# Plain scatters into rows of their own, the last two blocks summed from SBUF, and a head with two-column products

## The chip, the cores and the metric

One core of a Trainium2 chip runs the whole program once. The metric is device time in microseconds (us). The engines are TensorE (PE, matrix products), VectorE (DVE), ScalarE (ACT), GpSimd (POOL) and SyncE (SP, here mostly an issuer of transfers); 16 DMA engines move data between DRAM and on-chip memory (SBUF), for all queues together.

## What is computed

One layer of a decoder trunk on 1024 tokens of width 1024, all in float32: adaLN modulation, an input projection, dilated attention beside a depthwise convolution, an output projection, and then a mixture of experts, with a final norm:

```python
mod = silu(c) @ w_mod + b_mod                  # six vectors of 1024
h = rms_norm(x, g_norm1) * (1 + sc1) + sh1
u = h @ w_in                                   # q, k, v, ga, gb
x = x + gt1 * (concat([attention(q, k, v), conv(ga, gb)]) @ w_out)
h2 = rms_norm(x, g_norm2) * (1 + sc2) + sh2
# per token: one of 4 groups, in it the top 2 of 8 experts, weights w
x = x + gt2 * sum_over_the_two(w * (silu(h2 @ w_gate[e]) * (h2 @ w_up[e])) @ w_down[e])
out = rms_norm(x, g_final)
```

## The kernel before

**Head.** TensorE makes shift and scale of the first norm, two vectors in four halves of 512, as products of `ca` with blocks of w_mod (`mod_mm`, L129), lying in rows. To turn them into columns it multiplies by single columns of the identity: four halves j by eight k, 32 products of one column (L190). VectorE makes s1 and a1 of them (L192 to L194). Behind that `h_half` turns the normed x by 4 transposes for each of 8 k and two halves (L203), and ScalarE writes hT from them (L205).

**Projections and attention.** The products of hT with w_in go on from about 41 us (L268 to L270). POOL's queue loads further blocks of w_mod in that stage (L122). Then attention, convolution on VectorE, output projection, second norm and the routing tables follow, up to about 640 us.

**Experts.** 32 experts, sorted by load; each has three matrices of 2 MB. They pass through a ring of eight buffers of 2 MB (`ring` L578, `eload` L588): SP issues two loads of 1 MB for each matrix, in one fixed order (`uses`), and each issue waits for its buffer and for the transfer eight issues before. Experts in the list PK (13 of them, 64 tokens at most) use F32 products (L1035, L1104); the others split the weights into a rounded part and a rest on ScalarE and VectorE (L102, L105) and use three fp32r products each (L1046 to L1048, L1122 to L1124). For each expert POOL gathers the tokens' rows from `h2d` (`gather`, L931) and, at its end, `scatter` (L1089) adds the scaled result `ys` (L1135) into `x1d` in DRAM: an indirect transfer with `compute_op=OP.add`. Two tokens' experts may meet in a row of x1d, so each scatter waits for the one before. The order of TensorE, VectorE and ScalarE in this stage is written by hand; SP and POOL follow in program order.

**Overflow and end.** `tc.If(nov > j)` (L1360) covers experts with more tokens than fit; `nov` is 0 here, so the branch is not taken, but it stands in the program. After it, for each of 8 tiles of 128 tokens: SP loads a tile of x1d (L1390), ScalarE sums its squares (L1392), POOL makes 1/rms in two steps (L93, L94), VectorE scales (L1394), and ScalarE's queue writes it out (L1395).

Of the kernel before, what the change touches and what calls it, by code (L numbers as in the profile page):

```python
# [35 lines left out]
PK = (4, 6, 8, 10, 12, 14, 16, 18, 20, 23, 25, 28, 31)  # L36
C0, C1 = 2, 3
# [6 lines left out]
def trunk_kernel(ctx, tc, x, c, w_mod, b_mod, g_norm1, w_in, conv_w, conv_b, conv_ln_g, conv_ln_b,  # L44
# [15 lines left out]
    h2d = dram.tile([T, D], F32, name="h2d")  # L60
    x1d = dram.tile([T, D], F32, name="x1d")
# [124 lines left out]
    pc0 = pbank(psT)  # L186
# [5 lines left out]
    nc.vector.tensor_add(s1, pc0[:, 0:8], bm[:, 0, :])  # L192
    nc.vector.scalar_tensor_tensor(a1, pc0[:, 8:16], 1.0, bm[:, 1, :], op0=OP.add, op1=OP.add)
# [5 lines left out]
    def h_half(half):  # L199
        for k in range(8):  # L200
            pt = pbank(psT)
            for i in range(4):
                nc.tensor.transpose(pt[:, i * P:(i + 1) * P], xn[half * 4 + i][:, k:D:8], ident)  # L203
# [47 lines left out]
    modp = tc.alloc_tile_pool(name="modp", bufs=2, side="right")  # L251

# [457 lines left out]
    early_t, late_t = [[rtc.tile([P, n], dt, name=f"{nm}{n}") for nm, dt in (("ti", I32), ("ws", F32))]  # L710
                       for n in (LO, E - LO + 1 + NOV)]

    half_t = [rtc.tile([P, E - LO + 1], dt, name=f"{nm}h") for nm, dt in (("ti", I32), ("ws", F32))]
# [8 lines left out]
    def tables(tb, dst, pool, halves=False):  # L722

        ti, ws = dst
# [182 lines left out]
    gt2b = tabp.tile([P, D], F32, name="gt2b")  # L907
    caps = tabp.tile([E, 2], F32, name="caps")
    pos = tabp.tile([1, E + 1], I32, name="pos")
    ovr = tabp.tile([1, NOV], I32, name="ovr")  # L910
    moe = tc.alloc_tile_pool(name="moe", bufs=2, side="right", reuse_waits="tile")
# [12 lines left out]
    todo = []  # L924

# [163 lines left out]
    def scatter(ys, si, n):  # L1089

        nc.gpsimd.indirect_dma_start(  # L1091
# [4 lines left out]
    def down(e):  # L1096
# [359 lines left out]
```

## Time and profile before

| | us |
|---|---|
| median of 3 runs | 1183.0 (1182.07 to 1186.11) |
| the profiled execution | 1183.84 |
| its span | 1182.0 |
| TensorE busy | 1081.5 (91% of the span) |
| VectorE busy | 784.1 (66%) |
| ScalarE busy | 513.0 (43%) |
| POOL busy | 224.3 (19%) |

All times of the profile are in us from the span's start. TensorE is busy for most of the span, but the limits differ by stage: near the start it waits for w_mod, in the experts' stage all 16 DMA engines are busy, and at the end TensorE has nothing to do at all. A row of a timeline gives the start, the length, the engine (PEld is TensorE's weight load, an engine name with q its queue's sequencer), the line, the operation with output<-input, and the count of merged instructions.

### The profile page before, as it was taken

The page shows a single profiled execution, that of the slowest core. Times are in us where ns is not written, and L with a number is a line of the kernel's source. Part 1 is how long each engine was busy: PE and PEld are TensorE (multiplying, and loading weights), DVE is VectorE, ACT ScalarE, POOL GpSimd, SP SyncE. Part 2 cuts the span into 40 slices and gives each one's busy share as a digit, 9 for nine tenths or more (in the row PEclk, how much of TensorE's full clock was granted, in tenths as well). Part 3 has the DMA queues.
Part 4 walks back from the last instruction along what each step waited for, and adds up shares of the span by engine and source line. Part 5 has one row for each costly group of instructions (what it writes and reads, how often), then busy time and mean ns, then how long its engine had stood idle before and what let it go on. Part 6 is the DMA issues. An engine that isn't in the chain of part 4 may idle for free. (4 is left out here: it accounts for less than half of the span.)

```text
span 1182.0 us, 16081 instructions
## 1 busy us (share of the span) xinstructions
PE 1081.5 (91%) x5896; PEld 790.6 (67%) x5896; DVE 784.1 (66%) x1303; ACT 513.0 (43%) x800; POOL 224.3 (19%) x202
## 2 busy tenths in 40 slices
PE   3899999999799999999889999999979999898970
PEld 0667777778565666788678877777656677576740
DVE  1457999993666556777669766666654587485833
ACT  2431112111777665322257655554553475364613
POOL 2340000002412202300111222222111231221112
PEclk8799999999798999999979999999989999999995
DMA  9632634302011004744868999999999999999948
GB/s 367 207 139 94 240 116 145 111 30 89 1 37 36 1 1 173 287 183 162 324 222 302 357 398 408 406 399 384 392 391 384 386 389 369 380 402 373 395 129 294
DMA packets 60828, 292.65 MB, mean 248 GB/s; under 512 B 11861, under 2 KB 16213, under 8 KB 33092
## 3 DMA queue, kind: packets, MB, share of 16 engines
q1 hardware_dynamic: 48020, 253.16, 54.8%
q0 software_dynamic: 11296, 34.17, 10.1%
q10 hardware_dynamic: 1424, 4.20, 0.9%
q8 instruction: 48, 0.79, 0.3%
q14 instruction: 40, 0.33, 0.1%
HBM read 275.75 MB, written 26.23 MB: 255 GB/s over the span
## 5 line engine op out<-in xcount | busy, mean ns | idle before, releaser
L105 DVE TENSOR_TENSOR elo<-raw,ehi 128x1024 fp32r<-128x1024 f32 x228 | 271.0, 1221 | 91.9 <-ACT ehi L102 90.0
L102 ACT CAST ehi<-raw 128x1024 fp32r<-128x1024 f32 x228 | 234.1, 1049 | 98.9 <-DMA raw<-in_w_exp_down_dram 33.1
L317 DVE SCALAR_TENSOR_TENSOR cv<-cv,cwT 128x1024 f32<-128x1024 f32 x120 | 154.1, 1284 | 3.6
L269 PE MATMUL pb<-hT,whi 128*128 128x512 f32 x256 | 101.2, 395 | 1.7 <-POOL hT L98 1.3
L268 PE MATMUL pb<-hT,whi 128*128 128x512 f32 x256 | 102.5, 402 | 0.0
L270 PE MATMUL pb<-hT,wlo 128*128 128x512 f32 x256 | 101.0, 395 | 0.1
L1122 PE MATMUL py<-ehi,hh 128*128 128x512 f32 x152 | 64.5, 424 | 7.1 <-ACT ehi L102 5.6
L1091 POOL DMA_INDIRECT x1d<-ys,ti x19 | 42.6, 2240 | 132.3 <-DVE ys L1135 117.2
L1123 PE MATMUL py<-elo,hh 128*128 128x512 f32 x152 | 62.8, 413 | 2.7 <-DVE elo L105 2.6
L268 PEld LDWEIGHTS pb<-hT,whi 128*128 128x128 f32 x256 | 48.5, 189 | 21.9 <-ACT whi L102 9.2
L1124 PE MATMUL py<-ehi,hl 128*128 128x512 f32 x152 | 62.0, 408 | 0.9 <-DVE hl L105 0.9
L1046 PE MATMUL pg<-ehi,xh 128*128 128x512 f32 x152 | 61.6, 405 | 0.4 <-ACT xh L102 0.4
L1047 PE MATMUL pu<-elo,xh 128*128 128x512 f32 x152 | 60.2, 396 | 0.4 <-DVE elo L105 0.4
L1048 PE MATMUL pg<-ehi,xl 128*128 128x512 f32 x152 | 59.9, 394 | 0.3 <-DVE xl L105 0.3
L1046 PE MATMUL pu<-ehi,xh 128*128 128x512 f32 x152 | 59.9, 394 | 0.0
L1048 PE MATMUL pu<-ehi,xl 128*128 128x512 f32 x152 | 59.8, 393 | 0.0
L1047 PE MATMUL pg<-elo,xh 128*128 128x512 f32 x152 | 59.7, 393 | 0.0
L269 PEld LDWEIGHTS pb<-hT,whi 128*128 128x128 f32 x256 | 48.5, 190 | 13.1 <-POOL hT L98 2.9
L1035 PE MATMUL pu<-raw,x 128*64 128x256 f32 x448 | 51.6, 381 | 5.5 <-DMA raw<-in_w_exp_up_dram 5.5
L270 PEld LDWEIGHTS pb<-hT,wlo 128*128 128x128 f32 x256 | 48.5, 190 | 10.4 <-DVE wlo L105 0.6
L422 ACT ACTIVATE ns<-ns,st 128x128 f32<-128x128 f32 (+7 forms) x64 | 49.2, 772 | 11.1 <-DVE st L418 10.5
L931 POOL DMA_INDIRECT xe<-h2d,ti x20 | 29.5, 1474 | 128.0 <-PE pt L1015 90.1
(284 smaller groups left out, 2197.3 us busy)
## 6 DMA issues: line engine op xcount, KB each, us to landing
raw<-in_w_exp_gate_dram SPq DMA_DIRECT2D x64, 1024.0 KB, 22.6
raw<-in_w_exp_up_dram SPq DMA_DIRECT2D x64, 1024.0 KB, 23.4
raw<-in_w_exp_down_dram SPq DMA_DIRECT2D x64, 1024.0 KB, 22.8
wm<-in_w_mod_dram POOLq DMA_DIRECT2D x16, 1024.0 KB, 5.2
wm<-in_w_mod_dram SPq DMA_DIRECT2D x8, 1024.0 KB, 9.5
raw<-in_w_in_dram SPq DMA_DIRECT2D x3, 2048.0 KB, 9.8
xt<-in_x_dram SPq DMA_DIRECT2D x8, 512.0 KB
raw<-in_w_in_dram SPq DMA_DIRECT2D x4, 1024.0 KB, 12.6
```

The source lines that it names most:

```text
L102: nc.scalar.copy(hi, src)
L105: nc.vector.tensor_sub(lo, src, hi.bitcast(F32))
L268: nc.tensor.matmul(p[half], hi[:, k, :], hT[0][:, k, sl], start=(k == 0), stop=False)
L269: nc.tensor.matmul(p[half], hi[:, k, :], hT[1][:, k, sl], start=False, stop=False)
L270: nc.tensor.matmul(p[half], lo[:, k, :], hT[0][:, k, sl], start=False, stop=(k == 7))
L317: nc.vector.scalar_tensor_tensor(y, u[:, j:j + T], w, y, op0=OP.mult, op1=OP.add)
L1046: nc.tensor.matmul(o, xh[:, k, :], hi[:, kk, :], start=(k == 0), stop=False)
L1047: nc.tensor.matmul(o, xh[:, k, :], lo[:, kk, :], start=False, stop=False)
L1048: nc.tensor.matmul(o, xl[:, k, :], hi[:, kk, :], start=False, stop=(k == 7))
L1122: nc.tensor.matmul(o, hh[:, k, :], hi[:, half, :], start=(k == 0), stop=False)
L1123: nc.tensor.matmul(o, hh[:, k, :], lo[:, half, :], start=False, stop=False)
L1124: nc.tensor.matmul(o, hl[:, k, :], hi[:, half, :], start=False, stop=(k == 3))
```

## The change

Three parts.

**Head.** The 32 one-column products become 16 with two columns each (`ident[:, 32 * h:P:64]`), whose results land in neighbouring columns. Five of the first half's eight groups of transposes (`x_turned`) are placed by hand between the w_mod products.

**Scatters.** A new DRAM buffer `ybuf` has two rows per token, one for each chosen expert. It is zeroed in the projections' stage by eight transfers of 1 MB on POOL's queue from one small tile. A scatter now writes plainly to row 2*token + choice; the tables get a second index `si` for it. The scatters are declared independent of each other.

**End.** The results of the last two experts (30 and 31, `LATE`) are not scattered; they stay in SBUF, split into two fp32r parts, and one-hot matrices S (`late_tokens`) say which token each row belongs to. SP loads all of x1d (2 transfers of 2 MB) and ybuf (8 of 1 MB) into ring buffers behind the last weights, ahead of the branch. After the branch, for each tile: two rows of ybuf are added to x1d, on VectorE for even tiles (`fin_v`) or by F32 products with the identity on TensorE for odd ones (`fin_y`); eight fp32r products add the late results (`fin_late`); VectorE adds the sum from PSUM (`fin_add`), and square, 1/rms, scaling and the write follow (`fin_out`, the write on SP's queue).

```diff
@@ head
+    def x_turned(half, k, pool):
+        pt = pbank(pool)
+        for i in range(4):
+            nc.tensor.transpose(pt[:, i * P:(i + 1) * P], xn[half * 4 + i][:, k:D:8], ident)
+        return pt
-    for k in range(8):
-        mod_mm(pm, mod_load(nc.sync, xp, 0, k, 4), k)
+    with tc.manual_schedule(engines={mybir.EngineType.PE}):
+        for k in range(8):
+            mod_mm(pm, mod_load(nc.sync, xp, 0, k, 4), k)
+            if k > 2:
+                turned[0, k - 3] = x_turned(0, k - 3, ps1)
-    for j in range(4):
-        c0 = 8 * (j // 2)
-        for k in range(8):
-            nc.tensor.matmul(pc0[64 * (j % 2):64 * (j % 2) + 64, c0 + k:c0 + k + 1], mrow[:, k:512:8],
-                             ident[:, 32 * j:32 * j + 1], start=True, stop=True, skip_group_check=True)
+    for k in range(8):
+        for h in range(2):
+            nc.tensor.matmul(pc0[64 * h:64 * h + 64, 2 * k:2 * k + 2], mrow[:, k:512:8],
+                             ident[:, 32 * h:P:64], start=True, stop=True, skip_group_check=True)
...
@@ projections
+    zt = modp.tile([P, 256], F32, name="zt", bufs=1)
+    nc.gpsimd.memset(zt, 0.0)
+    for i in range(8):
+        nc.gpsimd.dma_start(ybuf.rearrange("(p r) (q d) -> p (r q) d", p=P, d=256)[:, 8 * i:8 * i + 8, :],
+                            zt[:, None, :].to_broadcast([P, 8, 256]))
...
@@ scatter
-        nc.gpsimd.indirect_dma_start(
-            out=x1d.rearrange("t (n f) -> (t n) f", n=n),
+        s = nc.gpsimd.indirect_dma_start(
+            out=ybuf.rearrange("t (n f) -> (t n) f", n=n),
             out_offset=bass.IndirectOffsetOnAxis(ap=si, axis=0),
-            in_=ys, in_offset=None, bounds_check=n * T - 1, oob_is_err=False, compute_op=OP.add)
+            in_=ys, in_offset=None, bounds_check=2 * n * T - 1, oob_is_err=False)
+        for o in scat:
+            tc.declare_no_dep(s.ins, o.ins, reason="each slot has its own row")
+        scat.append(s)
...
@@ down, late results
-            if i:
+            if i and e not in LATE:
                 scatter(ys, si, n)
+        if e in LATE:
+            todo.append(lambda: late_parts(e, ys))
+    def late_tokens():
+        r = mixp.tile([P, 4 * D], F32R, name="late0", tag="raw")
+        for i, e in enumerate(LATE):
+            S = r[:, i * D:(i + 1) * D].rearrange("p (t q) -> p t q", q=P)
+            late["S", e] = S
+            yield lambda i=i, S=S: v.tensor_tensor(S, iota[:, None, :].to_broadcast([P, 8, P]),
+                                                   tokm[:, i, :, None].to_broadcast([P, 8, P]), op=OP.is_equal)
+        late["r", LATE[0]] = r[:, 2 * D:]
+    def late_parts(e, ys):
+        if e == E - 1:
+            late_place()
+        w = ys.shape[-1]
+        hi, lo = late["h", e] = [late["r", e][:, i * D:i * D + w] for i in range(2)]
+        split(hi, lo, ys)
...
@@ behind the last expert
-    gfb = ring(7).rearrange("p k f -> p (k f)")[:, 0:D]
-    bcast(gfb, g_final[None, :])
+        fx = [ring(i).rearrange("p (t k) f -> p t (k f)", k=2) for i in (0, 1)]
+        for i, f in enumerate(fx):
+            nc.sync.dma_start(f, x1d[i * 512:i * 512 + 512, :].rearrange("(t p) d -> p t d", p=P))
+        yv = ybuf.rearrange("(t k) d -> t (k d)", k=2)
+        yt = [ring((2, 4, 5, 6)[tt // 2]).rearrange("p (t k a) f -> p t k (a f)", t=2, k=2)[:, tt % 2] for tt in range(8)]
+        def results():
+            for tt, y in enumerate(yt):
+                nc.sync.dma_start(y.rearrange("p k d -> p (k d)"), yv[tt * P:(tt + 1) * P, :])
+        results()
     nov = nc.values_load(pos[0:1, E:E + 1], min_val=0, max_val=NOV)
...
@@ inside the branch
+            if j == 0:
+                results()
@@ the end
-    for tt in range(8):
...
-        nc.sync.dma_start(f, x1d[ts, :])
+    gfb = tabp.tile([P, D], F32, name="gfb", tag="gt2b")
+    nc.gpsimd.dma_start(gfb, g_final[None, :].to_broadcast([P, D]))
+    def fin_y(tt):
+        pf = fsum[tt] = psf.tile([P, D], F32, name="pf")
+        for h in range(2):
+            for k in range(2):
+                nc.tensor.matmul(pf[:, 512 * h:512 * h + 512], ident, yt[tt][:, k, 512 * h:512 * h + 512],
+                                 start=(k == 0), stop=False, skip_group_check=True)
+    def fin_late(tt):
...
+        jobs = [(e, p) for e in LATE for p in range(2)]
+        for h in range(2):
+            for n, (e, p) in enumerate(jobs):
+                S, y = late["S", e], late["h", e][p]
+                ps, c0 = (slice(64 * h, 64 * h + 64), 0) if e in PK else (slice(0, P), 512 * h)
+                nc.tensor.matmul(pf[:, 512 * h:512 * h + 512], S[ps, tt, :], y[ps, c0:c0 + 512],
+                                 start=(new and n == 0), stop=(n == len(jobs) - 1), skip_group_check=True)
+    def fin_v(tt):
+        for k in range(2):
+            v.tensor_add(fin_x(tt), fin_x(tt), yt[tt][:, k, :])
+    def fin_add(tt):
+        f = fin_x(tt)
+        v.tensor_add(f, f, fsum[tt])
         fs = moe.tile([P, 1], F32, name="fst", bufs=4)
...
+        nc.scalar.activation(yt[tt][:, 1, :], f, AF.Square, accum_out=fs)
+        fr[tt] = rstd_of(moe, fs, 1, 1.0 / D)
+    def fin_out(tt):
+        q = yt[tt][:, 0, :]
+        v.scalar_tensor_tensor(q, fin_x(tt), fr[tt], gfb, op0=OP.mult, op1=OP.mult)
+        nc.sync.dma_start(out[tt * P:(tt + 1) * P, :], q)
+    with tc.manual_schedule(engines={mybir.EngineType.PE, mybir.EngineType.DVE, mybir.EngineType.Activation}):
+        fin_v(0)
+        for i in range(0, 8, 2):
+            fin_y(i + 1)
+            if i < 6:
+                fin_v(i + 2)
+            if i:
+                fin_out(i - 2)
+                fin_out(i - 1)
+            for t in (i, i + 1):
+                fin_late(t)
+                fin_add(t)
+        fin_out(6)
+        fin_out(7)
```

How the compiled order shows it, at three places. A row is the line, the operation, output<-input with the partitions x elements, and a count; in brackets what the instruction waits for (DMAHW0 to DMAHW7 are the counters of SP's transfers, DMASW those of POOL's).

TensorE at the head, before (L129 the w_mod products, L190 the one-column products, L203 the transposes, L268 and on the projections):

```order
L129 MATMUL pb<-wm,ca 32x512 x32
L190 MATMUL pb<-ident,mrow 64x1 x32
L203 MATMUL pb<-ident,xn 128x128 x16
L268 MATMUL pb<-hT_87,whi 128x512
L269 MATMUL pb<-hT_88,whi 128x512
L270 MATMUL pb<-hT_87,wlo 128x512
```

The same place after (L131 the w_mod products, L184 the transposes, L201 the two-column products):

```order
L131 MATMUL pb<-wm,ca 32x512 x16
L184 MATMUL pb<-ident,xn 128x128 x4
L131 MATMUL pb<-wm,ca 32x512 x4
L184 MATMUL pb<-ident,xn 128x128 x4
L131 MATMUL pb<-wm,ca 32x512 x4
L184 MATMUL pb<-ident,xn 128x128 x4
L131 MATMUL pb<-wm,ca 32x512 x4
L184 MATMUL pb<-ident,xn 128x128 x4
L131 MATMUL pb<-wm,ca 32x512 x4
L184 MATMUL pb<-ident,xn 128x128 x4
L201 MATMUL pb<-ident,mrow 64x2 x16
L184 MATMUL pb<-ident,xn 128x128 x12
```

Five groups of four transposes have moved between the w_mod products, and half the products that turn the vectors are left.

SP behind the last weights, before (L595 the last of the weights, L518 the load of g_final, L1360 the overflow branch):

```order
L595 DMA raw<-in_w_exp_down_dram 128x2048 [waits DMAHW1_49,DVE_49]
L1357 TENSOR_LOAD pos [waits DVE_49]
L1357 ISA x2
L518 DMA raw<-in_g_final_dram 128x1024 [waits DMAHW2_49,DMAHW0_49,PE_49]
L1360 COMPARE_AND_BRANCH
L1360 UNCONDITIONAL_BRANCH [waits SP_sequencer_49,DMAHW0_49,DMAHW1_49,DMAHW2_49,DMAHW3_49,DMAHW4_49,DMAHW5_49,DMAHW6_49,DMAHW7_49]
```

The same place after (L1428 the loads of ybuf, behind the two of x1d; L1435 the overflow branch):

```order
L1428 DMA raw<-ybuf 128x2048 [waits DMASW5_49,DMASW6_49,DMASW3_49,DMAHW4_49,DMASW2_49,DVE_49]
L1428 DMA raw<-ybuf 128x2048 [waits DMAHW5_49,DVE_49]
L1428 DMA raw<-ybuf 128x2048 [waits DMAHW6_49,PE_49]
L1428 DMA raw<-ybuf 128x2048 [waits DMAHW7_49,PE_49]
L1428 DMA raw<-ybuf 128x2048 [waits DMAHW0_49,DVE_49]
L1428 DMA raw<-ybuf 128x2048 [waits DMAHW1_49,DVE_49]
L1428 DMA raw<-ybuf 128x2048 [waits DMAHW2_49,PE_49]
L1428 DMA raw<-ybuf 128x2048 [waits DMAHW3_49,PE_49]
L1432 TENSOR_LOAD pos [waits DVE_49]
L1432 ISA x2
L1435 COMPARE_AND_BRANCH
L1435 UNCONDITIONAL_BRANCH [waits SP_sequencer_49,DMAHW0_49,DMAHW1_49,DMAHW2_49,DMAHW3_49,DMAHW4_49,DMAHW5_49,DMAHW6_49,DMAHW7_49]
```

The eight loads of ybuf, one on each counter, now stand ahead of the branch, whose block for the case that it is not taken waits for all eight counters in both kernels.

VectorE from the last block's scaling on, before (L1135 the scaling of block results, L1394 the final scaling):

```order
L1135 SCALAR_TENSOR_TENSOR ys<-py,ws_3605,gt2b 128x512
L1360 UNCONDITIONAL_BRANCH
L1394 SCALAR_TENSOR_TENSOR raw<-raw,rstd 128x1024 [waits DMAHW2_49,DMAHW3_49,DMAHW1_49,DMAHW5_49,DMAHW0_49,DMAHW7_49,Activation_49,Pool_49]
L1394 SCALAR_TENSOR_TENSOR raw<-raw,rstd 128x1024 [waits DMAHW2_49,DMAHW4_49,DMAHW0_49,DMAHW6_49,Activation_49,Pool_49]
L1394 SCALAR_TENSOR_TENSOR raw<-raw,rstd 128x1024 [waits DMAHW1_49,DMAHW5_49,DVE_49,DMAHW7_49,Activation_49,Pool_49]
```

The same place after (L1158 that scaling, L1494 the additions of `fin_v`, L1498 those of `fin_add`, L1505 the final scaling):

```order
L1158 SCALAR_TENSOR_TENSOR ys<-py,ws_3605,gt2b 128x512
L1435 UNCONDITIONAL_BRANCH x3
L1494 TENSOR_TENSOR raw<-raw 128x1024 [waits DMAHW4_49,DMAHW6_49,DMAHW2_49,DMAHW0_49]
L1494 TENSOR_TENSOR raw<-raw 128x1024 [waits DVE_49]
L1494 TENSOR_TENSOR raw<-raw 128x1024 [waits DMAHW4_49,DMAHW3_49,DMAHW0_49]
L1494 TENSOR_TENSOR raw<-raw 128x1024 [waits DVE_49]
L1498 TENSOR_TENSOR raw<-raw,pf 128x1024 [waits PE_49] x2
L1494 TENSOR_TENSOR raw<-raw 128x1024 [waits DMAHW6_49,DMAHW3_49]
L1494 TENSOR_TENSOR raw<-raw 128x1024 [waits DVE_49]
L1505 SCALAR_TENSOR_TENSOR raw<-raw,rstd,gfb 128x1024 [waits DMASW4_49,Activation_49,Pool_49]
```

Between the branch and the final scaling VectorE has the additions of ybuf's rows and of the sums from PSUM, and the first of them waits for counters of SP's transfers.

## Rows read from the trace of the kernel before

**Rows 1.** busy share of the 16 DMA engines in 40 slices, tenths (page)

```profile
DMA  9632634302011004744868999999999999999948
```

**Rows 2.** 640 to 1120 us by stretches: each engine's busy time, granted clock, DMA share, GB/s

```profile
820.00:880.00 60.00, 53.15 (x297) 36.53 (x294) 32.73 (x35) 25.92 (x32) 11.14 (x7) 0.94 1.01 388
...
1000.00:1060.00 60.00, 54.74 (x275) 38.83 (x274) 38.41 (x41) 30.33 (x38) 12.36 (x6) 0.97 1.02 392
1060.00:1120.00 60.00, 55.75 (x279) 41.13 (x278) 42.62 (x45) 34.51 (x42) 12.67 (x6) 0.97 1.01 386
sum 480.00, PE 462.68 PEld 335.22 DVE 319.46 ACT 252.28 POOL 103.48; mean PE 57.83 PEld 41.90 DVE 39.93 ACT 31.54 POOL 12.94
```

**Rows 3.** SP's own waits, 700 to 1122 us: us in total, times, longest

```profile
SPq L595 <- DMA raw<-in_w_exp_up_dram: 104.0, 42, 4.0
```

**Rows 4.** timeline of the end, from 1118 us: start us, us, engine, line, operation

```profile
1131.30 2.28 POOL L1091 DMA_INDIRECT x1d<-ys,ti  x1 [13.57 <-DVE ys L1135]
...
1133.40 0.63 PE L1122 MATMUL py<-ehi,hh 128*128 128x512 f32 x1
...
1133.83 0.63 PE L1123 MATMUL py<-elo,hh 128*128 128x512 f32 x1
...
1136.78 0.39 PE L1123 MATMUL py<-elo,hh 128*128 128x512 f32 x1
...
1137.00 0.39 PE L1124 MATMUL py<-ehi,hl 128*128 128x512 f32 x1
...
1144.60 3.65 PE L1104 MATMUL py<-raw,h 128*64 128x512 f32 x16 [0.46 <-ACT h L1083]
...
1150.27 1.57 POOL L1091 DMA_INDIRECT x1d<-ys,tih  x1 [6.95 <-DVEq L1360]
1156.98 5.07 SPq L1390 DMA_DIRECT2D raw<-x1d  x8
```

**Rows 5.** the chain that ended last: its last row

```profile
1176.76 1.28 DVE raw L1394
```

**Rows 6.** timeline of the head, 31 to 41 us

```profile
32.82 6.48 PE L190 MATMUL pb<-ident,mrow 128*64 128x1 f32 x64 [0.70 <-ACT mrow L185]
...
39.23 1.97 PE L203 MATMUL pb<-ident,xn 128*128 128x128 f32 x8
```

**Rows 7.** DMA of 30 to 46 us, all queues

```profile
DMA packets 4295, 5.87 MB, mean 367 GB/s; under 512 B 118, under 2 KB 3782, under 8 KB 4294
```

**Rows 8.** 72 to 130 us by stretches, columns as in group 2

```profile
72.00:100.00 28.00, 27.26 (x127) 19.05 (x126) 14.90 (x15) 6.79 (x9) 8.74 (x18) 1.00 0.59 206
100.00:130.00 30.00, 30.00 (x139) 23.00 (x138) 28.68 (x26) 3.19 (x4) 1.06 (x2) 1.00 0.41 138
```

**Rows 9.** DMA queues, 927.2 to 939.6 us, one scatter: packets, MB, share of 16

```profile
q0 software_dynamic: 144, 0.52, 21.3%
```

**Rows 10.** the same, 914.5 to 927.2 us, one gather

```profile
q0 software_dynamic: 144, 0.31, 6.4%
```

**Rows 11.** the same, 1162 to 1182 us, writes of out_dram on ScalarE's queue

```profile
q10 hardware_dynamic: 1152, 4.19, 51.4%
```

**Rows 12.** the same, 640 to 1122 us

```profile
q1 hardware_dynamic: 23582, 171.71, 88.7%
q0 software_dynamic: 7521, 14.71, 12.1%
```

**Rows 13.** waits of POOL, 640 to 1160 us: us in total, times, longest

```profile
POOL x1d L1091 <- DMA x1d<-ys,ti: 55.5, 8, 10.0
```

**Rows 14.** groups by line and shape: busy us, mean ns of one | idle before

```profile
L821 DVE TENSOR_TENSOR xr<-sc,xr 128x512 f32<-128x512 f32 x16 | 11.0, 690 | 12.8 <-PE sc L814 12.7
...
L1394 DVE SCALAR_TENSOR_TENSOR raw<-raw,rstd 128x1024 f32<-128x1024 f32 x8 | 10.3, 1285 | 18.0 <-DMA raw<-x1d 13.0 <-POOL rstd L94 4.3 <-DMA out_dram<-raw 0.7
...
L839 DVE TENSOR_TENSOR h<-h,sh2b 128x1024 f32<-128x1024 f32 x7 | 8.6, 1224 | 0.1
...
L1392 ACT ACTIVATE raw<-raw 128x1024 f32<-128x1024 f32 x8 | 8.5, 1057 | 21.9 <-DMA raw<-x1d 16.1 <-POOL rstd L93 3.4 <-DVE raw L1394 2.4
```

More of the change, by code (lines that the diff above doesn't have):

```diff
@@ L60, in trunk_kernel @@
     h2d = dram.tile([T, D], F32, name="h2d")
+    ybuf = dram.tile([2 * T, D], F32, name="ybuf")
     x1d = dram.tile([T, D], F32, name="x1d")
@@ L200, in h_half @@
         for k in range(8):
-            pt = pbank(psT)
-            for i in range(4):
-                nc.tensor.transpose(pt[:, i * P:(i + 1) * P], xn[half * 4 + i][:, k:D:8], ident)
+            pt = turned.pop((half, k), None) or x_turned(half, k, psT)
             sl = slice(half * 512, half * 512 + 512)
@@ L707, in onehots @@
         return o
-    early_t, late_t = [[rtc.tile([P, n], dt, name=f"{nm}{n}") for nm, dt in (("ti", I32), ("ws", F32))]
+    early_t, late_t = [[rtc.tile([P, n], dt, name=f"{nm}{n}") for nm, dt in (("ti", I32), ("si", I32), ("ws", F32))]
                        for n in (LO, E - LO + 1 + NOV)]
-    half_t = [rtc.tile([P, E - LO + 1], dt, name=f"{nm}h") for nm, dt in (("ti", I32), ("ws", F32))]
+    half_t = [rtc.tile([P, E - LO + 1], dt, name=f"{nm}h") for nm, dt in (("ti", I32), ("si", I32), ("ws", F32))]
     tb = rtc.tile([P, 4, 2, E], F32, name="tb")
@@ L906, in trunk_kernel @@
     tabp = tc.alloc_tile_pool(name="tabp", bufs=1, side="right", reuse_waits="tile")
-    gt2b = tabp.tile([P, D], F32, name="gt2b")
+    gt2b = tabp.tile([P, D], F32, name="gt2b", tag="gt2b")
     caps = tabp.tile([E, 2], F32, name="caps")
@@ L910, in trunk_kernel @@
     ovr = tabp.tile([1, NOV], I32, name="ovr")
+    tokm = tabp.tile([P, len(LATE), 8], F32, name="tokm")
     moe = tc.alloc_tile_pool(name="moe", bufs=2, side="right", reuse_waits="tile")
@@ L1110, in down @@
             if e == E:
[L1111 removed]
+                si, ws = [t[:, E - LO:E - LO + 1] for t in half_t[1:]]
             else:
[L1113 removed]
+                si, ws = slots(e)[1:]
             w, n = 512, 2
@@ L1317, in trunk_kernel @@
         table = position_tables()
+        rows = late_rows()
         next(table)
@@ L1333, in trunk_kernel @@
                 run(table)
+                todo.extend([lambda: next(rows, None)] * 3)
             nxt = steps(e + 1) if e + 1 < E else []
@@ L1383, in trunk_kernel @@
     psx.release()
-    for tt in range(8):
-        ts = slice(tt * P, (tt + 1) * P)
-        y = ring(2 + tt // 2).rearrange("p (t k a) f -> p t k (a f)", t=2, k=2)[:, tt % 2]
-        f, q = y[:, 0, :], y[:, 1, :]
-        nc.sync.dma_start(f, x1d[ts, :])
-        fs = moe.tile([P, 1], F32, name="fst", bufs=4)
-        nc.scalar.activation(q, f, AF.Square, accum_out=fs)
-        r = rstd_of(moe, fs, 1, 1.0 / D)
-        nc.vector.scalar_tensor_tensor(q, f, r, gfb, op0=OP.mult, op1=OP.mult)
-        nc.scalar.dma_start(out[ts, :], q)
+    psf = tc.alloc_tile_pool(name="psf", bufs=4, space=PSUM, reuse_waits="tile")
@@ new lines, in trunk_kernel @@
+    gfb = tabp.tile([P, D], F32, name="gfb", tag="gt2b")
+    nc.gpsimd.dma_start(gfb, g_final[None, :].to_broadcast([P, D]))
+    fr, fsum = {}, {}
+    def fin_y(tt):
[5 more added lines that the diff above has]
+    def fin_late(tt):
+        new = tt not in fsum
+        pf = fsum[tt] if not new else psf.tile([P, D], F32, name="pf")
+        fsum[tt] = pf
+        jobs = [(e, p) for e in LATE for p in range(2)]
[5 more added lines that the diff above has]
+                                 start=(new and n == 0), stop=(n == len(jobs) - 1), skip_group_check=True)
```

41 lines of the change are left out of this document (33 added, 8 removed).

## The prediction

> **What bounds the kernel now.** I read the page's forty slices first. The row of the DMA engines says where the limit lies: single digits that change up to slice 22, then nines from slice 23 to slice 38, that is from about 650 to 1122 us, the stage in which the expert weights pass through eight buffers [rows 1]. The table by stretches says what this does to TensorE: its busy time over 640 to 1120 us is 462.68 of 480 us, so 17.3 us are idle, and 16.4 of them lie in three stretches from 820 us on; there the mean granted clock is 0.94, 0.97 and 0.97, so 60 x 0.06 + 2 x 60 x 0.03 = 7.2 us worth of clock are gone as well [rows 2]. The queue's own waits say who is late: SP waits for earlier transfers to land, 104.0 us for the up matrices alone [rows 3]. So the transfers set the pace there, just, and TensorE is close behind: with no late weight at all the stage would end 17.3 + 7.2 = 24.5 us sooner and no more.
>
> The end is another limit. TensorE's last product starts at 1144.60 and ends at 1148.25; call that T0. The scatter of block 31 goes out at 1150.27, SP can read x1d at 1156.98 when that has landed [rows 4], the last scaling ends at 1176.76 + 1.28 = 1178.04 [rows 5], and the span at 1182.0, 3.96 later and T0 + 33.75. The profiled execution took 1183.84, 1.84 more than its span and 0.84 above the median of 1183.0; my sum is made against 1183.84.
>
> **Head.** The 32 one-column products are recorded as 64 instructions, 6.48 us, and the transposes start behind them at 39.23 [rows 6]. Sixteen two-column products are half the instructions: -3.24 us. Five groups of transposes move in between the w_mod products, where TensorE waits for weights. Only the first of them stands before ScalarE's first hT; eight took 1.97 us [rows 6], so a group of four 1.0, and a part of that lies beside VectorE's small steps on s1 and a1: -0.6. Together -3.85 at most. I take -3.
>
> **Zero fill.** 8.39 MB of zeros are new, on POOL's queue behind the first w_mod load of the projections (75 us). In 30 to 46 us, where nearly all packets were under 2 KB, 367 GB/s were moved [rows 7]: about 23 us of transfer. The stretches around it have room: DMA is busy 0.59 of 72 to 100 us and 0.41 of 100 to 130 [rows 8], so 28 x 0.41 + 30 x 0.59 = 29 us are free, and TensorE is busy 27.26 of 28 and 30.00 of 30 us there, on weights that are there already. The next w_mod loads stand behind the zeros on POOL's queue; their products stand behind more projection products in the new order. I take 0, and 10 us for the case that a weight comes late.
>
> **Plain scatters.** No view shows one, so I bound it. Above: an accumulating scatter cost, in a stretch with one of them and nothing else on that queue, 21.3% of 16 engines for 12.4 us, 42.3 engine-us for 0.52 MB, 81 us per MB [rows 9]. Below: a gather on the same queue, row by row as a plain scatter, 6.4% of 12.7 us, 13.0 engine-us for 0.31 MB, 42 us per MB [rows 10]; writes of out_dram took 51.4% of 20 us for 4.19 MB, 39 us per MB [rows 11]. A plain scatter is nearest to these two. Over the whole stage the queue moved 14.71 MB in 12.1% of 482 us [rows 12], 933 engine-us; gathers are about half of it, and 7.2 MB x 42 + 7.5 MB x 81 = 910 agrees. So 7.5 MB x (39 to 42) is 290 to 315 engine-us, over 16 engines **18 to 20 us** of transfer time, 0.6 us per scatter. If it costs what it did, the gain is 0.
>
> How much of that reaches T0? At 860 us, 220 of 482 us into the stage, 0.46 of it is in hand, 8 to 9 us: more than the 6.85 us of idle time in 820 to 880 [rows 2]. At 1120 it is 17 to 19, as much as the 17.3. So most of the idle time goes, and some of the half-clock time with it; a few waits for ScalarE and VectorE, which hang on no transfer, stay. I take **-16**, bounds 0 and -24.5, likely -8 to -22. POOL waits less too: 55.5 us of its time were waits of a scatter for the one before [rows 13]. Its gathers stand behind them, but ahead of TensorE's need, so this is 0 on its own.
>
> The Trainium skill bears on that wait: "DMA: Bandwidth & Descriptors", Rules for kernel authors, says of an accumulating transfer beside another access of the same bytes that it has to wait for the earlier one's semaphore, or additions are lost. The trace of before agrees (the 55.5 us); with a row of its own for each pair of token and choice nothing needs to wait.
>
> **The end.** Before: T0 + 33.75. After, the scatter of 31, its landing and the load of x1d leave the path; three things come in.
>
> (a) 8.39 MB of ybuf and 4.19 MB of x1d where 4.19 MB were read. By the order the first ybuf load waits for all scatters up to 29. That of 29 was issued at 1131.30, T0 - 17, and the last one took 6.7 us from issue to x1d being readable [rows 4], so T0 - 10, or T0 - 9 beside other traffic. In front of ybuf on SP stand the last weights and x1d; the DMA row's slice from 1123 to 1152 shows 0.4 [rows 1], so x1d has room there. From T0 - 9 the 8.39 MB at 186.4 MB in 482 us, 0.39 MB per us [rows 12], need 21.5 us, and 1.5 more for landing and what is left of x1d: **T0 + 14**. If x1d gets no room ahead, T0 + 20; at best T0 + 12.
>
> (b) Nothing starts until they have all landed. The order shows it: the block that SP runs when the overflow branch is not taken waits for all eight of its transfer counters and then moves them on, and the first addition (VectorE) and the first product (TensorE) of the sums wait for counts that this block sets. Before, the same block stood ahead of the x1d loads, beside the last scatter, and cost nothing. So the loads stand ahead of the branch, but the sums do not overlap them.
>
> (c) The sums. Per odd tile four F32 products with the identity: L1104's eight (16 records) took 3.65 us, two side by side on halves of the array, 0.91 for each pair [rows 4]; I take 0.95, 3.8 a tile, 15.2 for four. Per tile eight fp32r products at the interval of 0.22 us [rows 4]: 1.8, and 14.5 for eight. TensorE has been idle for over 10 us by then; after a wait at 1132 its products stand 0.43 us apart in place of 0.22, its lower clock level of 1.2 GHz [rows 4], so +1.7. Sum 31.4 us. VectorE beside it: 8 additions of 1.22, 8 from PSUM at 0.69 per half, some 1.3, and 8 scalings of 1.285 [rows 14]: 30 us, in step with it. The last pair then needs two additions from PSUM, a square of 1.06, POOL's two small steps (0.9) and a scaling: 4.7, and 4 for the last write as before. So 31.4 + 4.7 + 4 = **40.1 us** from the landing to the end.
>
> End after: T0 + 14 + 40.1 = T0 + 54.1, 20.4 more than 33.75. Bounds: T0 + 12 and 38 us (every price at its lower end), +16; T0 + 20 and 43, +29.
>
> Here the skill's rule would give another time: the same page and section has it that a transfer issued early and waited for late overlaps with compute. The new end issues early; its order waits early as well. What the rule gives if it held is the third rival.
>
> **Sum.** 1183.84 - 3 - 16 + 20.4 = 1185.2; with a little for the zero fill, which can take a part of the head's gain back, I say **1186**.
>
> **Rivals.**
> 1. Faster, by full relief. All 24.5 us come back, the head keeps 3.85, and the loads land at T0 + 12, since the queue is further ahead: 1183.84 - 3.85 - 24.5 + 18.4 = 1173.9. For it: 16.4 of 17.3 idle us lie after 820 us, when the queue's lead is used up, and 0.6 us per scatter would keep the lead. Against: the relief (17 to 19) just covers the idle time and leaves nothing for the clock. It decides from -22 in the stage on.
> 2. Slower: the plain scatter costs the engines as much as the accumulating one. Gain 0 to 3 in the stage: 1183.84 - 3 - 2 + 20.4 = 1199. For it: a scatter's rows are as small and scattered as before, and the queue is the same. Against: the two prices [rows 10, 11]. It decides from a saving under 0.3 us per scatter.
> 3. The sums start with the first tiles, at T0 + 4 (block 31's split), and end 40.1 us later: +10.4, and 1175. Against: the order.
> 4. The zero fill makes a projection weight late by 10 us: 1196.
>
> **How the numbers follow.** Forecast 0.58 (1178 to 1194 by its own bounds; a seventh of it under 1179.5, a third over 1186.5), rival 1 0.15, rival 2 0.10, rival 3 0.07, rival 4 0.10. 0.3% of 1183 is 3.5 us, about what a measurement of this kernel can tell from no change. Faster: rivals 1 and 3 and 0.08 of the forecast, 0.30. Slower: rivals 2 and 4 and 0.20 of the forecast, 0.40. Same: the rest, 0.30. The range leaves the ends of rivals 1 and 2 and half of the forecast's tails out: 1174 to 1199.
>
> **What would show it.** After: TensorE's idle time from 640 us to T0 near 2 to 5 us instead of 17.3, with no stretch's clock under 0.97; the POOL queue's share near 8% of the stage instead of 12.1%; no wait of POOL for a scatter. At the end SP's wait in the branch's block until about T0 + 14, the first work of the sums on TensorE and VectorE right behind it, and 40 us from there to the end. At the head, sixteen products in about 3.2 us. The step on the end is wrong if the first sum starts before the last ybuf load lands, or if TensorE stays at 1.2 GHz through the sums, which would add up to 25 us; the step on the scatters, if the queue's share doesn't fall.

## The result

The changed kernel takes 1200.6 us (1198.7 to 1201.7) where the kernel before takes 1182.5 in the same runs: ratio 1.0143, 95% interval 1.0122 to 1.0165. It is slower by 18 us, on the side that the forecast leaned to, but beyond the upper end of the range (1199). The profiled execution has a span of 1198.8 us against 1182.0.

Four marks divide the two spans: the first projection product, the experts' first product (L1046, after L1067), TensorE's last expert product (its end is T0), and the end.

| | before | after | after - before |
|---|---|---|---|
| first projection product starts | 42.8 | 36.8 | -6.0 |
| first expert product starts | 601.1 | 602.4 | +1.3 |
| from there to T0 | 547.1 | 525.0 | -22.2 |
| T0 | 1148.2 | 1127.3 | -20.9 |
| from T0 to the end of the span | 33.8 | 71.5 | +37.7 |

So the head gains 6 us and loses them again before the experts start, the experts' stage gains 22 us, and the end costs 38.

**The experts' stage**, by stretches (columns as in [rows 2]: TensorE's busy time first, then at the end of a row its granted clock, the DMA share, GB/s):

```profile
820.00:880.00 60.00, 58.83 (x354) 41.65 (x354) 38.62 (x42) 31.60 (x39) 9.38 (x9) 1.00 1.01 408
...
1000.00:1060.00 60.00, 59.38 (x329) 42.96 (x329) 40.42 (x44) 31.10 (x38) 12.92 (x9) 1.00 1.01 408
1060.00:1120.00 60.00, 56.04 (x292) 41.01 (x290) 45.48 (x47) 33.55 (x41) 7.45 (x4) 1.00 0.97 394
sum 480.00, PE 473.50 PEld 346.51 DVE 336.94 ACT 260.94 POOL 87.67; mean PE 59.19 PEld 43.31 DVE 42.12 ACT 32.62 POOL 10.96
```

TensorE is idle for 6.5 us of 480 where it was 17.3, the clock is at 1.00 throughout, and the transfers run at 408 GB/s in the first two of these rows where [rows 2] has 388 and 392. The queues of 640 to 1122 us say why (packets, MB, share of 16 engines; [rows 12] before):

```profile
q1 hardware_dynamic: 24886, 178.59, 91.6%
q0 software_dynamic: 6912, 15.22, 8.2%
```

POOL's queue moves slightly more than before, 15.22 MB, in 8.2% of the engines' time where 14.71 MB took 12.1%: 301 engine-us less, 18.8 us of the 16 together. SP's queue fills that room.

Over the whole stage, from the first expert product to T0, TensorE has the same 2878 product records (before, then after):

```profile
601.12:1148.25 547.13, 524.53 (x2878) 381.60 (x2878) 361.29 (x408) 284.62 (x344) 110.42 (x63) 0.98 0.97 368
```

```profile
602.37:1127.33 524.96, 514.65 (x2878) 376.57 (x2878) 366.90 (x424) 286.32 (x345) 89.80 (x62) 0.99 0.98 391
```

Its idle time falls from 22.6 to 10.3 us, and its busy time by 9.9 at a higher mean clock: together the 22.2.

**The end**, from the timeline of 1110 to 1200 us (start, length, engine, line, operation, what ended the wait before it):

```profile
1111.67 1.71 POOL L1111 DMA_INDIRECT ybuf<-ys,si  x1 [13.54 <-DVE ys L1158]
...
1121.36 9.36 SPq L1428 DMA_DIRECT2D raw<-ybuf  x8
...
1123.68 3.65 PE L1127 MATMUL py<-raw,h 128*64 128x512 f32 x16 [0.52 <-ACT h L1104]
...
1153.39 4.88 DVE L1494 TENSOR_TENSOR raw<-raw 128x1024 f32<-128x1024 f32 x4 [23.08 <-SPq L1435]
...
1153.47 5.52 PE L1473 MATMUL pf<-raw,ident 128*128 128x512 f32 x8 [26.14 <-SPq L1435]
...
1158.42 1.04 PE L1486 MATMUL pf<-late 128*128 128x512 f32 x2
...
1159.39 0.73 PE L1486 MATMUL pf<-late,late 64*128 64x512 f32 x2
```

The scatter of block 29 goes out at 1111.67. The first ybuf load waits for it until 1121.36, T0 - 6. Block 31's last product ends at 1127.33, and from there TensorE does nothing and VectorE almost nothing for 26 us. At 1153.4 both start at once, and both rows name the same releaser: SP's block at L1435, the branch that isn't taken. SP's transfers in that stretch:

```profile
GB/s 184 256 368 389 445 389 424 445 404 430 424 419 440 389 409 419 384 450 378 404 394 378 409 384 460 419 419 419 338 225 194 205 174 143 102 113 51 41 20 0
...
q1 hardware_dynamic: 1461, 9.60, 73.4%
```

Forty slices of 0.8 us: from the fourth to the 28th the queue runs at some 410 GB/s, and in the last third it fades out, 338, 225, 194, 205 and so on down to 20. The last load lands at 1153.0. SP's own waits (us in total, times, longest) show what held the loads back:

```profile
SPq L1428 <- DMA ybuf<-ys,si: 15.7, 1, 15.7
SPq L1428 <- DMA raw<-x1d: 5.6, 2, 4.7
```

The first row is the scatter. The second holds the last two ybuf loads until x1d has landed, so the last one goes out only at 1130.4, T0 + 3. Each load moves its counter in sixteen steps, and the trace has the time of each. x1d's second load, issued at 1104.1, had eight steps by 1115.6, one at 1122.0 and the last seven from 1127.1 to 1130.3. The last ybuf load had its first seven by 1145.0 and its last seven from 1148.3 to 1153.0. So nearly half of the steps were late before the first ybuf load was issued, and they were still late at the end.

The chain of waits of the whole span then has nothing but the sums:

```profile
1153.47 5.52 PE pf L1473 x8
1158.99 5.11 PE pf L1486 x16
1164.10 3.63 PE pf L1473 x8
1167.73 5.09 PE pf L1486 x16
...
1185.17 4.95 PE pf L1486 x16
...
1193.69 1.28 DVE raw L1505
```

Four times 8 records of F32 products (3.63 us, the first 5.52) and 16 fp32r products (5.1 us, two tiles): 36.6 us of TensorE, and 8.7 from there to the end.

### The profile page after: what moved, and what is told of

Its sections match the earlier page's. It is cut to its first block, busy times and chain, and to the rows that moved or that the text cites. A ratio compares the mean times of both kernels' runs of the same rounds, so it can differ in the third digit from the quotient of the medians.

```text
span 1198.8 us, 16246 instructions
## 1 busy us (share of the span) xinstructions
PE 1107.0 (92%) x5960; PEld 798.0 (67%) x5960; DVE 808.7 (67%) x1338; ACT 515.0 (43%) x802; POOL 211.7 (18%) x210
## 5 line engine op out<-in xcount | busy, mean ns | idle before, releaser
L1067 PE MATMUL pg<-ehi,xh 128*128 128x512 f32 x152 | 61.1, 402 | 0.5 <-ACT xh L104 0.5
L1146 PE MATMUL py<-elo,hh 128*128 128x512 f32 x152 | 59.7, 393 | 1.2 <-DVE elo L107 1.2
L1067 PE MATMUL pu<-ehi,xh 128*128 128x512 f32 x152 | 59.9, 394 | 0.0
L433 DVE CUSTOM_DVE_ANT_0 ns<-sc,raw 128x384 f32<-128x384 f32 (+5 forms) x64 | 33.4, 536 | 31.8 <-PE sc L430 18.0
L1111 POOL DMA_INDIRECT ybuf<-ys,si x18 | 31.5, 1748 | 126.5 <-DVE ys L1158 119.9
```

What stands on the lines that cost most here:

```text
L1067: nc.tensor.matmul(o, xh[:, k, :], hi[:, kk, :], start=(k == 0), stop=False)
L1146: nc.tensor.matmul(o, hh[:, k, :], lo[:, half, :], start=False, stop=False)
```

## The experiments

All variants are edits of the changed kernel unless said otherwise. The ratio compares each with the kernel before on the same chip, where that one took 1182.5 us (beside the changed kernel), 1183.9 (e1 to e4), 1185.4 (e5 to e7) and 1184.3 (e8, e9); medians of different groups differ by that much without any edit. The marks are those of each profiled run:

| kernel | first expert product | from there to T0 | T0 to the end | median, us | ratio to before |
|---|---|---|---|---|---|
| before | 601.1 | 547.1 | 33.8 | 1182.5 | 1 |
| after | 602.4 | 525.0 | 71.5 | 1200.6 | 1.0143 |
| e1 head alone | 594.5 | 547.1 | 35.3 | 1175.7 | 0.9921 (0.9895 to 0.9948) |
| e2 zeros later | 593.2 | 526.1 | 70.2 | 1191.4 | 1.0063 (1.0045 to 1.0080) |
| e3 accumulating | 603.3 | 546.1 | 73.4 | 1224.3 | 1.0343 (1.0323 to 1.0363) |
| e4 each waits | 604.9 | 523.9 | 72.2 | 1202.0 | 1.0150 (1.0133 to 1.0167) |
| e5 loads behind the branch | 601.5 | 525.9 | 60.5 | 1190.0 | 1.0039 (1.0022 to 1.0057) |
| e6 late products by expert | 606.1 | 526.3 | 65.7 | 1196.9 | 1.0104 (1.0078 to 1.0130) |
| e7 combined | 591.8 | 523.8 | 54.9 | 1174.1 | 0.9921 (0.9896 to 0.9946) |
| e8 branch without SP's loads | 604.0 | 526.2 | 53.3 | 1187.2 | 1.0022 (1.0002 to 1.0043) |
| e9 combined, loads ahead | 590.1 | 526.2 | 51.0 | 1169.4 | 0.9874 (0.9821 to 0.9926) |

The column from the first expert product to T0 has just two values, 546 to 547 where the scatters add and 524 to 526 where they write plainly. With the new head and the zeros in their early place the first expert product wanders between 601 and 606; in the four kernels that have the new head and the zeros later or not at all (e1, e2, e7, e9) it stands at 590 to 595.

### e1: the head alone, on the kernel before

The edit is the head's part of the diff, with the lines for the scatters and the end as before.

> The kernel before with the head's part alone: 16 two-column products, five groups of transposes between the w_mod products; scatters and end as before. In the changed kernel the first projection product starts 6.0 us sooner (36.8 for 42.8) and the last one 6.6 us sooner, but the experts' first gather 1.2 us later; its convolution on VectorE starts at 120 us instead of 84. Theory (the zero fill's place in the program moves the convolution behind other work, and that eats the head's gain): here the convolution starts by 80 us and the gain stays, 1182.5 - 5 to 6.5, so 1176 to 1178. Rival (attention and the output projection have their own pace and swallow whatever the head gives): 1181 to 1183.

1175.7 us (1173.1 to 1178.8), a gain of 8 us. In the profiled execution, the slowest of the four, 6.2 us of it stand at the first projection product (36.6 for 42.8) and 6.6 at the first expert product, and the convolution starts by 76 us. The theory holds, and the gain is larger than the head's own instructions explain. The stretches of TensorE at the head say where it comes from, first before, then e1:

```profile
24.00:32.00 8.00, 6.03 (x28) 0.60 (x24) 0.00 (x0) 0.00 (x0) 0.00 (x0) 0.50 1.03 391
32.00:41.00 9.00, 8.30 (x76) 8.17 (x73) 0.41 (x3) 1.20 (x2) 0.00 (x0) 0.50 1.06 381
```

```profile
24.00:32.00 8.00, 6.06 (x48) 2.55 (x40) 0.00 (x0) 0.42 (x1) 0.00 (x0) 1.00 1.02 390
32.00:41.00 9.00, 6.08 (x52) 4.58 (x51) 5.07 (x9) 6.34 (x10) 1.27 (x1) 0.98 1.06 381
```

Before, TensorE ran at a granted clock of 0.50 from 24 to 41 us, at 1.2 GHz; the w_mod products had waits of 0.5 to 1.4 us between them. With the transposes in these gaps the clock is 1.00 and 0.98 in the same stretches, 2.4 GHz, and the 32 records of the two-column products take 2.09 us where the 64 took 6.48.

### e2: the zeros later

```diff
-    zt = modp.tile([P, 256], F32, name="zt", bufs=1)       # ahead of the gates
...
+    zt = modp.tile([P, 256], F32, name="zt", bufs=1)       # behind the last mod_next
...
```

> The changed kernel with the eight zero fills written behind the last w_mod loads of the projections (some 215 us) instead of ahead of the first gate. Theory (zeros' place moves the convolution): VectorE's first convolution operation at about 80 us, the experts' first gather some 6 us sooner (590 for 596), time 1200.6 - 6, about 1194 to 1195. Rival (the head's own new order of TensorE delays the convolution, or nothing of it reaches the end): 1199 to 1201.

1191.4 us, 9 less than the changed kernel where I expected 6, and the first expert product at 593.2. The zeros did not go out at 215 us, as I had expected. POOL's timelines, the changed kernel and then e2:

```profile
68.71 7.09 POOL L265 DMA_DIRECT2D ybuf<-zt  x8
```

```profile
79.52 0.97 POOL L316 DMA_DIRECT2D ybuf<-zt  x1
...
112.64 0.90 POOL L316 DMA_DIRECT2D ybuf<-zt  x1
```

They went out between the w_mod loads, from 79.5 to 113.5 us, and the DMA engines were as busy from 90 to 120 us as in the changed kernel (share 0.97 for 0.92). What changed is the order on VectorE. Its first convolution operations, from the timelines of the changed kernel and of e2:

```profile
118.66 0.69 DVE L301 TENSOR_TENSOR cv<-pb,cv 128x512 f32<-128x512 f32 x1 [4.73 <-PE pb L285]
119.26 0.81 DVE L330 TENSOR_SCALAR cv<-cv,cwT 128x1024 f32<-128x1024 f32 x1
120.11 2.60 DVE L332 SCALAR_TENSOR_TENSOR cv<-cv,cwT 128x1024 f32<-128x1024 f32 x2
```

```profile
75.04 0.81 DVE L330 TENSOR_SCALAR cv<-cv,cwT 128x1024 f32<-128x1024 f32 x1
75.89 3.93 DVE L332 SCALAR_TENSOR_TENSOR cv<-cv,cwT 128x1024 f32<-128x1024 f32 x3
```

So it was the place of the zeros in the program. No weight came late enough to matter: TensorE's last projection product stands at 245.6 in the changed kernel and at 244.4 here. But with the zeros in the early place, the order that the scheduler chose for VectorE put the convolution 44 us later, behind a multiplication that waits for TensorE, and its last operation at 302.4 instead of 266.0, into the attention's time.

### e3: scatters that add; e4: plain scatters that wait

```diff
@@ e3
-            ..., bounds_check=2 * n * T - 1, oob_is_err=False)
+            ..., bounds_check=2 * n * T - 1, oob_is_err=False, compute_op=OP.add)
@@ e4
-        for o in scat:
-            tc.declare_no_dep(s.ins, o.ins, reason="each slot has its own row")
```

> The changed kernel whose scatters add into the zeroed rows (an accumulating transfer) as in the kernel before, but independent of each other. Theory (the accumulation costs the 16 DMA engines twice the time of a plain write): the POOL queue's share of the experts' stage is back at about 12% from 8.2%, TensorE's idle time there at 15 us or more, its last product about 20 us later, time 1215 to 1222. Rival (what cost time before was each scatter's wait for the one before): time stays at 1199 to 1203.

> The changed kernel with plain scatters that each wait for the one before (no declaration of independence). Theory (price of accumulation): 1199 to 1203, as the changed kernel, since POOL has nothing urgent behind a scatter. Rival (the waits): 1213 to 1222, with POOL waiting some 50 us in all for its scatters.

1224.3, a little above the 1215 to 1222 that I expected, and 1202.0. The accumulation is the price: with it, but without the waits, the stage takes 546.1 us, 1.1 less than before. The waits cost nothing that can be told apart. POOL's queue of 640 to 1122 us in e3 (e4 has the row of the changed kernel again, 15.22 MB in 8.2%):

```profile
q0 software_dynamic: 7456, 14.59, 11.8%
```

e3 also has the idle time back, and in two of the three stretches the clock of 0.97 (in 820 to 880 us it is at 1.00 where it was 0.94):

```profile
1000.00:1060.00 60.00, 54.43 (x276) 38.95 (x277) 38.83 (x41) 30.98 (x37) 13.03 (x7) 0.97 1.01 388
1060.00:1120.00 60.00, 55.52 (x280) 41.72 (x279) 42.50 (x46) 34.60 (x42) 12.43 (x6) 0.97 1.01 386
sum 480.00, PE 459.54 PEld 332.82 DVE 319.36 ACT 252.48 POOL 101.56; mean PE 57.44 PEld 41.60 DVE 39.92 ACT 31.56 POOL 12.69
```

In e4 POOL waits for a scatter just once for long, where [rows 13] had 55.5 us: a plain one has landed before the next is due.

```profile
POOL ybuf L1111 <- DMA ybuf<-ys,si: 8.9, 1, 8.9
```

### e5: the ybuf loads behind the branch

```diff
-        results()                    # behind the last expert, ahead of the branch
...
-            if j == 0:
-                results()            # inside the branch
...
+    results()                        # behind overflow(0)
```

> The changed kernel with the ybuf loads written behind the overflow branch instead of ahead of it; the sums as they are. T0 is the end of TensorE's last expert product (1127.3 in the changed kernel; all ybuf loads have landed at T0 + 26, the sums start there and the span ends at T0 + 71.5). Theory (the block of the branch not taken makes the sums wait for all loads): the loads now start only when all engines have passed the branch, about T0 + 3 instead of T0 - 6, but the first sum starts with the first tile, about T0 + 8, and the end is set by TensorE's 36.6 us of sums: T0 + 53, time 1182. Rival (the loads themselves are the limit, each waits for the slowest DMA engine): first sum not before T0 + 25, time 1199 or more.

1190.0, so 10.6 less; I expected 18. The edit moves x1d's two loads as well, but the compiled program still issues them ahead of the branch, at 1099.5 and 1102.6; only the ybuf loads moved. These start at T0 + 4.7, and the first sum with the first tile, but that is there 7 us after its issue, not 5, and the first product comes only at T0 + 14.2:

```profile
1132.10 5.50 SPq L1452 DMA_DIRECT2D raw<-ybuf  x8
1139.12 2.48 DVE L1492 TENSOR_TENSOR raw<-raw 128x1024 f32<-128x1024 f32 x2 [8.69 <-DMA raw<-ybuf]
...
1141.64 4.60 PE L1471 MATMUL pf<-raw,ident 128*128 128x512 f32 x5 [14.20 <-DVE raw L1492]
```

The direction is the theory's: the end needs 60.5 us instead of 71.5 although the loads start 10.7 us later against T0. It doesn't separate the wait from the fading of the queue, for here x1d has landed, at 1128.7, before the ybuf loads start. e8 does. But e5 says something of the fading. The queue's rate in 40 slices of 0.65 us from 1132 us:

```profile
GB/s 208 365 252 246 378 378 378 391 416 416 391 378 403 441 429 416 403 416 416 429 454 466 416 416 403 403 441 403 454 416 416 441 429 378 189 50 25 0 0 0
```

The same eight loads, and the rate holds until the 34th slice and is gone three slices later; the sixteen steps of the last load lie between 1154.3 and 1156.4. So a queue that runs dry need not fade. In the changed kernel the fading goes with the lag that x1d's loads had already.

### e8: the same loads, the same order, but no wait for all

```diff
-            eid = nc.values_load(..., engines=[mybir.EngineType.SP], ...)
+            eid = nc.values_load(..., engines=[mybir.EngineType.Pool], ...)
-                wt[e, i] = eload(wsrc(e, i, eid), slot=(2, 4, 5)[i])
+                wt[e, i] = eload(wsrc(e, i, eid), eng=nc.gpsimd, slot=(2, 4, 5)[i])
-                results()
+                results(nc.gpsimd)
```

The edit touches only the branch's body, which isn't run here. Since SP's counters aren't moved in there any more, the block for the other case has no wait for them.

> The changed kernel with one edit: the loads inside the overflow branch (not run here) are issued by POOL instead of SP. The compiled block for the branch not taken then holds no wait for SP's transfer counters any more, and the ybuf loads stay ahead of the branch. Theory (that block made the sums wait for all loads): the first sum on TensorE or VectorE now starts when the first tiles have landed, at T0 + 12 to T0 + 18 instead of T0 + 26, so 8 to 14 us less: 1187 to 1193. Rival (the tiles all land together at the end, since every load waits for the slowest DMA engine): the first sum at T0 + 24 or later, time 1198 to 1201.

1187.2, 13.4 less than the changed kernel, and from T0 to the end 53.3 us instead of 71.5. The first sum starts at T0 + 7.5, released by a ybuf load and not by SP's block:

```profile
1137.71 5.70 PE L1473 MATMUL pf<-raw,ident 128*128 128x512 f32 x8 [7.46 <-DMA raw<-ybuf]
...
1139.12 4.88 DVE L1494 TENSOR_TENSOR raw<-raw 128x1024 f32<-128x1024 f32 x4 [5.89 <-issue]
```

The loads run as in the changed kernel: issued from T0 - 7.7 to T0 + 1.5, landed from T0 + 4.0 to T0 + 24.2. I had expected the first sum at T0 + 12 to T0 + 18; the first tiles are there sooner. With the loads nearly the same and the wait gone, 18 us of the 37.7 are shown to be the wait for all of them. The rest is the first tiles' landing and the sums.

### e6: the late products by expert

```diff
-        jobs = [(e, p) for e in LATE for p in range(2)]
-        for h in range(2):
-            for n, (e, p) in enumerate(jobs):
+        for e in LATE:
+            for h in range(2):
+                for p in range(2):
```

> The changed kernel with the eight products for the late results ordered by expert (four of 128 rows, then four of 64) instead of switching after every pair. In the changed kernel they stand 0.33 us apart where the experts' products stand 0.22 apart. Theory (the switch between 128 and 64 rows costs the difference): 0.24 us apart, 8 tiles x 8 x 0.09 = 5.8 us less in the sums, time 1195. Rival (these products cost 0.33 in any order): 1200 to 1201.

1196.9, so 3.8 less; from T0 to the end 65.7 us, 5.8 less, as expected (the first expert product of its profiled run came 3.7 us later, long before the edited place). Two tiles' products, which took 5.1 us in the changed kernel:

```profile
1162.21 1.50 PE L1486 MATMUL pf<-late 128*128 128x512 f32 x4
1163.64 0.73 PE L1486 MATMUL pf<-late,late 64*128 64x512 f32 x4
1164.30 1.20 PE L1486 MATMUL pf<-late 128*128 128x512 f32 x4
1165.43 0.73 PE L1486 MATMUL pf<-late,late 64*128 64x512 f32 x4
1166.09 2.41 PE L1473 MATMUL pf<-raw,ident 128*128 128x512 f32 x5
```

From 1162.21 to 1166.09, 3.9 us. So the old order had cost time, but the price isn't the 0.09 of my theory on each: the four products of 64 rows follow each other in 0.66 us, 0.17 apart, those of 128 rows 0.28 (second tile). That the switch of the row count is the cause isn't shown: by the code, block 31's products use rows 0 to 63 for one half of the columns and rows 64 to 127 for the other, and the edit also puts these two beside each other. No run separates the two.

### e7 and e9: versions that put it together

e7 has the zeros later, the loads behind the branch, the late products by expert and ahead of the rows' products, and tile 7's rows on VectorE. e9 has the same sums, with e8's edit in place of e5's:

```diff
         for i in range(0, 8, 2):
-            fin_y(i + 1)
-            if i < 6:
-                fin_v(i + 2)
...
+            fin_late(i)
+            fin_late(i + 1)
+            if i + 1 in YP:          # YP = (1, 3, 5)
+                fin_y(i + 1)
+            fin_v(i)
+            if i + 1 not in YP:
+                fin_v(i + 1)
...
```

> The changed kernel with four edits: zeros written later, ybuf loads behind the branch, late products ordered by expert and ahead of the ybuf rows' products (so that they need no load), and tile 7's rows added on VectorE instead of TensorE. If the three theories hold: the experts' stage starts 6 us sooner, the sums on TensorE take some 30 us from T0 + 4 and the last tile ends at about T0 + 46: 1200.6 - 6 - 25 = 1169 to 1173, faster than the kernel before. If the loads are the limit: T0 + 60, 1183 to 1188.

> As the combined kernel before (zeros later, late products by expert and ahead of the rows' products, tile 7 on VectorE), but with the ybuf loads ahead of the branch and the branch's own loads on POOL, so that nothing waits for all of them. If loads can overlap both the last expert's products and the sums: the loads start at T0 - 7 instead of T0 + 6.6, end of the span at T0 + 43 to 48 instead of T0 + 54.9, time 1162 to 1167. If the ring with x1d in front makes the tiles late again: T0 + 52 to 55, 1171 to 1175.

1174.1 and 1169.4: both beat the kernel before, e9 by 1.3% (0.7 to 1.8), and e9 is the fastest of all. e7 comes near its 1169 to 1173 by luck: its end takes 54.9 us where I had 46, and its experts start 10.6 us sooner where I had 6. e9's end takes 51.0 us, not 43 to 48: T0 to the first row of VectorE is 9 us, and then VectorE is nearly in one piece until the last scaling at 1162.18, with a gap of 3.4 us for TensorE's sum of the first odd tile and several of 0.4 to 1.0 us for POOL's 1/rms:

```profile
1125.32 2.48 DVE L1497 TENSOR_TENSOR raw<-raw 128x1024 f32<-128x1024 f32 x2 [5.98 <-issue]
...
1132.54 1.22 DVE L1501 TENSOR_TENSOR raw<-raw,pf 128x1024 f32<-128x1024 f32 x1 [3.42 <-PE pf L1475]
...
1137.79 1.28 DVE L1508 SCALAR_TENSOR_TENSOR raw<-raw,rstd,gfb 128x1024 f32<-128x1024 f32 x1 [0.44 <-POOL rstd L96]
...
1162.18 1.28 DVE L1508 SCALAR_TENSOR_TENSOR raw<-raw,rstd,gfb 128x1024 f32<-128x1024 f32 x1 [0.71 <-POOL rstd L96]
```

So even the best of these ends is 17 us longer than that of the kernel before, and it pays only because the experts' stage is 21 us shorter and begins 11 us sooner. The head alone (e1, ratio 0.9921) gives as much as all of e7; the plain scatters with their best end add some 0.5% to it in e9, no more than the intervals leave open.

## Why the prediction was wrong

By its own sum, 1183.84 - 3 - 16 + 20.4, against what was measured, 1183.84 + 1.3 - 22.2 + 37.7 = 1200.6:

1. **Head, -3: wrong on both sides.** The head gave 6.0, not 3.85 at most, since I counted instructions at the duration of the row and didn't see that the row was a row at half the clock, which the transposes' new places would end [rows 6]. And all of it was lost again, 7.3 us, in a step that I had at 0, the zero fill. I looked for its cost on the DMA engines and in late weights. Rival 4, with 10 us, is near in size, but its mechanism isn't the one: e2 shows the loss in VectorE's order, where the convolution had moved back. That could have been read from the order: on VectorE the first convolution row stands behind five multiplications of the gates (L301) where it stood behind two. I had compared the orders only at the places where I expected a cost.

2. **Plain scatters, -16: right in mechanism and place, too low.** The price from the three neighbours [rows 9 to 11] held: 18.8 us of transfer time against 18 to 20, the share of 8% against "near 8%". 22.2 us reached T0, because the clock came back as well: over the whole stage 12.3 us less idle and 9.9 less busy on the same products. Of the 24.5 that I gave as the limit nearly all came: for this stage rival 1 was right, and with it the step that took 2 to 3 us off for waits on ScalarE and VectorE was wrong, and so was a number that left nothing for the clock, although the text gave some of it back. Rival 2 falls with e3.

3. **The landing, T0 + 14: the step that failed most, it was T0 + 26.** I took the scatter's landing from a lone one at the end, 6.7 us, plus one; in full traffic it took 9.7, and the loads started at T0 - 6, not T0 - 9. And I read the slice's DMA share of 0.4 as room for x1d [rows 1]. It was no room. x1d's loads went out 26 and 23 us ahead of T0 and landed only at T0 - 2 and T0 + 3, and the last two ybuf loads waited for them. With [rows 12]'s rate the 9.6 MB that the queue still had need 25 us, which would be T0 + 19; the rest, 7 us, goes with the late steps. e5 shows these loads without x1d beside them, and there they don't fade. Why nearly half of the steps lag stays open.

4. **Nothing starts until all have landed: right.** VectorE's and TensorE's first rows name SP's block, and e8 takes it away for 18.2 us. The Trainium skill's rule ("DMA: Bandwidth & Descriptors", Rules for kernel authors) asks for an early issue and a late wait; the order had the wait early, so the sums of the changed kernel got nothing from it. e8 has both, and its end is T0 + 53.3: the rule agrees with the trace there. That is 9 us later than rival 3's T0 + 44, for 3.5 us in the first tile's landing and 5.4 in the price of the next point.

5. **The sums, 40.1: 45.5.** The late products stood 0.33 us apart, not 0.22: their four pieces of the chain take 20.2 us where I had 14.5. I took the interval of products that all have 128 rows [rows 4]. e6 gets 5.8 of it back.

The end's own upper bound, +29, was too low: T0 + 20 for a landing of T0 + 26, and 43 us for sums of 45.5. That the time lies only 1.6 us beyond the range is luck, since the scatters gave 6 us more than I had taken.

## What to carry to other kernels

A load that is issued ahead of a branch isn't ahead of the work behind it if the branch's body uses the same transfer counters: the block for the case not taken waits for all of them, and a trace names that block as releaser. Price an accumulating transfer by the queue's share per MB beside that of a plain one; here a stage at the transfers' limit got all of that price back, and clock besides. A DMA share below one isn't room by itself: in e5 it stood at 0.4 to 0.5 from 1114.5 to 1125 us, and x1d's loads, issued at 1099.5 and 1102.6, still weren't through. When an edit adds instructions to a stage whose order a scheduler makes, read every engine's order there, not only those that run the new work.

## What the runs showed of the hardware that was not expected

- Short work in TensorE's gaps pays for more than itself: five groups of transposes between the w_mod products (0.7 us each, the first 1.1) lifted the granted clock from 0.50 to 1.00 in 24 to 32 us, and the products behind them took 2.09 us for 32 records instead of 6.48 for 64.
- The parts of one load can land far apart: seven of the sixteen steps of x1d's second load came some 12 to 15 us behind the first eight, and the ybuf loads behind it ended at a rate that fell over 9 us from 338 to 20 GB/s. The eight of them landed 11.5 to 25.2 us after their issue; in e5, with x1d landed before, 6.8 to 19.2, and all steps of a load came within some 2 us.
- fp32r products that change between 128 and 64 rows after every pair stood 0.33 us apart; grouped by rows, and with the two halves of the 64-row products side by side, they stood 0.28 and 0.17 apart.
